# Low key halves on all 128 rows, a second gate ahead of the first branch product, and the mask step's minimum written into the statistics

## The chip, the cores and the metric

The kernel runs on one core of one Trainium2 chip. The metric is the device time of one execution in microseconds (us); lower is better. The version before takes 1885.06 us, the median of three runs (1883.31 to 1887.6). What a measurement of this kernel can tell from no change is about 0.2%, 3.8 us.

## The reference, cut to what matters

One decoder layer over 1024 tokens of width 1024, in float32. The part that the change touches is the mixer:

```python
s = einsum('nbqhgd,nbkhd->nbhgqk', qb, kw) * (dh ** -0.5)     # dh = 64, blocks of 128
s = where(mask, s, NEG_INF)
m = max(s, axis=-1)
if sink is not None: m = maximum(m, sk)                       # the sliding-window heads
p = exp(s - m[..., None])
denom = sum(p, axis=-1)                                       # + exp(sk - m) with a sink
o = einsum('nbhgqk,nbkhd->nbqhgd', p, vw) / denom
...
merged = sigmoid(ga) * ya + sigmoid(gb) * yb                  # ya, yb: branch products of the two attentions
y = einsum('btd,de->bte', merged, w_o)
```

There are 16 query heads of a sliding-window attention with two key heads and sinks (branch A), and 24 heads of a dilated attention in three patterns (branch B). A normalisation, a SwiGLU feed-forward part and a second normalisation follow.

## The kernel before, in words

**Products in three passes.** TensorE multiplies float32 operands as float32r, so every operand is split into a high part (ScalarE's copy, `w_hi`, `kh`, ...) and a low part (VectorE's difference, `w_lo`, `kl`, ...). A product is the three passes hi·hi, hi·lo, lo·hi; `mac`, with lines 137, 138 and 139, issues them for one 128x512 result.

**Stages.** The prologue (to about 77 us) makes the modulated input `u`. Stage 1 (to about 823 us) projects `u` and runs attention. Stage 2 (to about 1110 us) makes the gates, the branch products and their merge. Then follow `w_o`, the normalisation, and the feed-forward part. In each stage TensorE carries the work, in the order in which the Python code issues it; every other engine's queue, SyncE's DMA queue (SP) among them, is in program order as well.

**Stage 1.** `units` holds 12 units of branch B (a pair of heads and a pattern) and then 8 of branch A. `stream` is a generator of projections: per B unit a key projection (`k_stacks`), a value projection and a query projection, eight steps each; per A unit a query projection, and in the first of them the shared values and keys too. The main loop goes over the units' four parts (`subs`, 80 in all); in each it calls `scores`, pumps some steps of projection, calls `turn_probs` for the part before (transposes, line 544), `exponentials` (line 522), pumps more steps, and calls `weigh` for the part two back (line 567). So TensorE's projections for later units lie between the pieces of attention. `tasks` sends the B units' statistics off and fetches the weights that combine the three patterns.

**Key stacks.** When a key projection has been rotated, `k_stacks` makes for each of the two heads a tile `kh` of 128 rows: the high part of the key in the head's own 64 rows (line 448) and the same again in the other 64 rows (line 449), both by ScalarE. The query stack `qs` holds the query's high part in the head's own 64 rows and its low part in the other 64. One product `qs`·`kh` over 128 rows (line 495) is thus (q_hi + q_lo)·k_hi. The low key `kl` is made by VectorE in the head's own 64 rows only (line 454); the product over those 64 rows (line 501) adds q_hi·k_lo. Only branch A's shared keys have the low part in both halves (line 456).

**Scores.** Per part there are two blocks and two heads: four products of line 495, then four of line 501, the heads' halves in turn. They are 256 columns wide, or 128 where a block sees no block before it. Of the 80 groups 36 are all 256 wide, 28 have two blocks' products of each width, and 16 are all 128 wide. VectorE then scales, masks and takes the row maximum in one `tensor_tensor_reduce` for each head and block (line 507) into a small tile `mx`; a `tensor_scalar` for each head (line 514, with the sink's maximum line 512) negates it into the statistics `st`; ScalarE's exponential takes `st` as its bias.

**Stage 2.** `order` lists gates ("g") and branch products ("w"): gate 8, products 0 to 7, gate 9, product 8, gate 10, product 9, and so on. A gate is 48 matmuls of `u` and two pieces of `w_in`, then tanh (line 675) and a scale by VectorE (line 676). A branch product is 24 matmuls of `o_hl`, the split attention output, and one piece of weights. Gates 11, 12 and 13 are made in stage 1 and kept in `ga_d` in HBM; `make_gate` only fetches them. Ahead of gate 8, `ws.prepare(4)` splits four pieces of weights and `o_parts(0)` splits the first four parts of attention output; while gate 8 runs no weights are split. While a gate or product runs, `ws.step` splits the next piece and a step of `ada_steps` (a modulation by VectorE, line 826 and line 828) runs.

## Time and profile before

| | |
|---|---|
| median of three runs | 1885.06 us |
| profiled execution, its own time | 1886.68 us |
| its span in the trace | 1884.6 us |
| TensorE busy | 1827.5 us, 97% of the span |
| VectorE, ScalarE, GpSimd busy | 1154.8, 784.0, 600.0 us |
| mean granted TensorE clock | 0.992 |

PE is TensorE's matmul, PEld its weight load, DVE VectorE, ACT ScalarE, POOL GpSimd, SP SyncE. A row of the timeline gives the start, the time from first start to last end, engine, line, operation, output and inputs, size and count, and in brackets the idle time before it and what ended that. Matmuls overlap in their pipeline, so the distance of two starts tells what one costs, and the shown length does not.

### The profile page before, as it was taken

The page shows a single profiled execution, that of the slowest core. Times are in us where ns is not written, and L with a number is a line of the kernel's source. Part 1 is how long each engine was busy: PE and PEld are TensorE (multiplying, and loading weights), DVE is VectorE, ACT ScalarE, POOL GpSimd, SP SyncE. Part 2 cuts the span into 40 slices and gives each one's busy share as a digit, 9 for nine tenths or more (in the row PEclk, how much of TensorE's full clock was granted, in tenths as well). Part 3 has the DMA queues.
Part 4 walks back from the last instruction along what each step waited for, and adds up shares of the span by engine and source line. Part 5 has one row for each costly group of instructions (what it writes and reads, how often), then busy time and mean ns, then how long its engine had stood idle before and what let it go on. Part 6 is the DMA issues. An engine that isn't in the chain of part 4 may idle for free.

```text
span 1884.6 us, 24305 instructions
## 1 busy us (share of the span) xinstructions
PE 1827.5 (97%) x8924; PEld 1475.4 (78%) x8924; DVE 1154.8 (61%) x2136; ACT 784.0 (42%) x1664; POOL 600.0 (32%) x389
## 2 busy tenths in 40 slices
PE   6899999999999999989999999999999999999998
PEld 3678887877878767768888878878888888888886
DVE  5865567667667887643645365575565444674567
ACT  3544454544454667743112132653433333421122
POOL 2422323223223312100312242455664333531223
PEclk9999999999999999999999999999999999999999
DMA  8211112112111132144543223122222222442222
GB/s 280 91 34 35 35 36 79 40 39 76 42 57 63 41 95 76 57 168 155 208 137 137 79 72 134 57 90 101 85 78 85 89 79 89 151 134 71 97 84 89
DMA packets 72408, 171.85 MB, mean 91 GB/s; under 512 B 13089, under 2 KB 14177, under 8 KB 72290
## 3 DMA queue, kind: packets, MB, share of 16 engines
q1 hardware_dynamic: 71954, 169.26, 26.3%
q8 instruction: 70, 1.15, 0.3%
q0 software_dynamic: 336, 1.06, 0.2%
q14 instruction: 48, 0.39, 0.1%
HBM read 146.33 MB, written 23.95 MB: 90 GB/s over the span
## 4 chain that ended last, share of the span: by engine, by line
PE 81%; DVE 9%; ACT 4%; issue 3%; POOL 2%; DMA 1%; DVEq 0%; SPq 0%; POOLq 0%; ACTq 0%
PE pf L1108 22%; PE pj L137 7%; PE pj L139 7%; PE pj L138 6%; PE p L138 5%; PE p L139 5%; PE p L137 5%; PE pf L138 5%; PE pf L139 5%; PE pf L137 5%; PE pt L544 2%; PE po L567 2%; PE s L495 1%; PE s L501 1%; DVE probs L507 1%
## 5 line engine op out<-in xcount | busy, mean ns | idle before, releaser
L137 PE MATMUL pj<-u,w_hi 128*128 128x512 f32 x720 | 301.1, 418 | 0.0
L139 PE MATMUL pj<-u,w_lo 128*128 128x512 f32 x720 | 283.7, 394 | 0.0
L138 PE MATMUL pj<-u,w_hi 128*128 128x512 f32 x720 | 282.5, 392 | 0.0
L419 POOL TENSOR_TENSOR rb<-rb,sin_t 128x512 f32<-128x512 f32 x64 | 86.7, 1355 | 502.5 <-DVE rb L417 438.0
L118 DVE TENSOR_TENSOR w_lo<-r,w_hi 128x512 fp32r<-128x512 f32 x110 | 116.2, 1059 | 138.8 <-ACT w_hi L117 137.8
L79 DVE TENSOR_TENSOR w_lo<-w_raw,w_hi 128x512 fp32r<-128x512 f32 x148 | 131.2, 890 | 85.2 <-ACT w_hi L78 83.0
L522 ACT ACTIVATE probs<-probs,st 128x128 f32<-128x128 f32 (+1 forms) x320 | 146.0, 460 | 59.3 <-DVE st L512 30.1
L137 PEld LDWEIGHTS pj<-u,w_hi 128*128 128x128 f32 x720 | 136.2, 189 | 33.4 <-issue 4.7
L139 PEld LDWEIGHTS pj<-u,w_lo 128*128 128x128 f32 x720 | 135.8, 189 | 30.4
L138 PEld LDWEIGHTS pj<-u,w_hi 128*128 128x128 f32 x720 | 136.5, 190 | 22.4
L138 PE MATMUL pf<-wd,h 128*128 128x512 f32 x352 | 137.1, 389 | 0.0
L139 PE MATMUL pf<-wd,h 128*128 128x512 f32 x352 | 137.1, 389 | 0.0
L137 PE MATMUL pf<-wd,h 128*128 128x512 f32 x352 | 137.1, 389 | 0.0
L62 POOL TENSOR_TENSOR w_raw<-w_raw,gate 128x512 f32<-128x512 f32 x60 | 85.5, 1439 | 143.9 <-DMA w_raw<-in_w_down 120.6
L1327 DVE SCALAR_TENSOR_TENSOR zt<-zt,pf 128x512 f32<-128x512 f32 x112 | 75.3, 685 | 79.7 <-PE pf L139 79.7
L420 POOL TENSOR_TENSOR r<-ra,rb 128x512 f32<-128x512 f32 x63 | 114.5, 1817 | 6.1 <-DVE kl L454 1.3
L78 ACT ACTIVATE w_hi<-w_raw 128x512 fp32r<-128x512 f32 x148 | 90.8, 624 | 33.9 <-PE p L138 16.8
L546 ACT ACTIVATE ptsb<-pt 128x512 f32<-128x512 f32 (+1 forms) x128 | 63.5, 547 | 93.4 <-PE pt L544 93.0
L137 PE MATMUL p<-o_hl,w_hi 128*128 128x512 f32 x192 | 76.1, 396 | 6.8 <-ACT o_hl L117 6.8
L137 PE MATMUL p<-u,w_hi 128*128 128x512 f32 x208 | 82.2, 395 | 0.0
L139 PE MATMUL p<-u,w_lo 128*128 128x512 f32 x208 | 81.1, 390 | 0.0
L138 PE MATMUL p<-u,w_hi 128*128 128x512 f32 x208 | 81.0, 389 | 0.0
(305 smaller groups left out, 4266.8 us busy)
## 6 DMA issues: line engine op xcount, KB each, us to landing
w_raw<-in_w_in SPq DMA_DIRECT2D x116, 256.0 KB
r<-in_w_gate_up SPq DMA_DIRECT2D x47, 512.0 KB
a_raw<-in_w_ada SPq DMA_DIRECT2D x32, 512.0 KB
w_raw<-in_w_down SPq DMA_DIRECT2D x44, 256.0 KB
h_raw<-h_d SPq DMA_DIRECT2D x22, 512.0 KB
h_d<-g SPq DMA_DIRECT2D x40, 256.0 KB
wa<-in_w_ada_m SPq DMA_DIRECT2D x16, 512.0 KB
wb<-wt_d SPq DMA_DIRECT2D x24, 256.0 KB
```

Source lines behind the costliest of these rows:

```text
L62: self.nc.gpsimd.tensor_tensor(self.raws[i], self.raws[i], scale(), op=OP.mult)
L78: self.nc.scalar.activation(hi, raw, AF.Copy)
L79: self.nc.vector.tensor_tensor(lo, raw, hi, op=OP.subtract)
L118: nc.vector.tensor_tensor(lo, src, hi, op=OP.subtract)
L137: nc.tensor.matmul(ps, w[0], m[0], start=first, stop=False)
L138: nc.tensor.matmul(ps, w[0], m[1], start=False, stop=False)
L139: nc.tensor.matmul(ps, w[1], m[0], start=False, stop=last)
L419: eng.tensor_tensor(b, b, sin_t[:, s], op=OP.mult)
L420: eng.tensor_tensor(residue_half(res, r, t), by_residue(a, r), by_residue(b, r), op=OP.add)
L522: nc.scalar.activation(pr, pr, AF.Exp, bias=st[:, 0, h, b:b + 1], accum_out=st[:, 1, h, b:b + 1])
L1108: nc.tensor.matmul(ps, w[:, c], m[:, k], start=first and k == 0 and n == 0, stop=k == 3 and n == 2, skip_group_check=True)
L1327: nc.vector.scalar_tensor_tensor(z, z, ALPHA if gi == 0 else 1.0, pd, op0=OP.mult, op1=OP.add)
```

## The change

Five edits.

1. `k_stacks` makes the high and the low key in the head's own 64 rows only, and two DMAs on SP's queue copy each into the other 64 rows. ScalarE's second copy (line 449) and VectorE's line 456 are gone. `kl` is a tile for each head, with four buffers.
2. `scores` multiplies the whole `qs` of 128 rows by `kl`, so that a part has eight products of 128 rows; high and low stand next to each other for each head and block. This adds q_lo·k_lo to the sum.
3. The mask step scales by -QS and reduces by the minimum, straight into `st`. For branch A the negated sink (`nsinks`, made once) is the reduction's start. `mx` and the two `tensor_scalar` are gone.
4. The exponential takes its input times -1.
5. Gate 10 is made after gate 8, ahead of product 0, and written to `ga_d`; where it stood, it is fetched. Its two pieces of weights come earlier in the list. It runs no step of `ada_steps`.

```diff
+    bridge = 10
...
+        if i == 0:
+            order.append(("b", bridge))
         order.append(("w", i))
     for kind, i in order:
-        if kind == "g" and i not in made_early:
+        if kind == "b" or (kind == "g" and i not in (*made_early, bridge)):
             add_chunk(I["w_in"][gate_of[i]], 2, 4)
...
             kh = att.tile([P, T], F32R, name="kh", bufs=4)
+            kl = att.tile([P, T], F32R, name="kl", bufs=4)
             nc.scalar.activation(kh[own], res[own], AF.Copy)
-            nc.scalar.activation(kh[other], res[own], AF.Copy)
+            nc.sync.dma_start(kh[other].bitcast(F32), kh[own].bitcast(F32))
+            nc.vector.tensor_tensor(kl[own], res[own], kh[own], op=OP.subtract)
+            nc.sync.dma_start(kl[other].bitcast(F32), kl[own].bitcast(F32))
...
-                nc.tensor.matmul(pss[h][:, i, lo:], box["q"][h][:, b * P:(b + 1) * P],
-                                 khs[h][:, (b - 1 + lo) * P:(b + 1) * P], start=i == 0, stop=False,
-                                 skip_group_check=True)
-
-        for i, b, lo in blocks:
-            for h, own in enumerate((LO, HI)):
-                nc.tensor.matmul(pss[h][:, i, lo:], box["q"][h][own, b * P:(b + 1) * P],
-                                 kls[h][own, (b - 1 + lo) * P:(b + 1) * P], start=False, stop=i == 1,
-                                 skip_group_check=True)
+                for n, ks in enumerate((khs, kls)):
+                    nc.tensor.matmul(pss[h][:, i, lo:], box["q"][h][:, b * P:(b + 1) * P],
+                                     ks[h][:, (b - 1 + lo) * P:(b + 1) * P], start=i == 0 and n == 0,
+                                     stop=i == 1 and n == 1, skip_group_check=True)
...
-                    out=probs[:, h, i, lo:], in0=pss[h][:, i, lo:], in1=un["mask"][:, lo:], scale=QS, scalar=NEG,
-                    op0=OP.add, op1=OP.max, accum_out=mx[:, h, i:i + 1])
-            sl = slice(2 * qr, 2 * qr + 2)
-            if "kv" in un:
-                nc.vector.tensor_scalar(st[:, 0, h, sl], mx[:, h], un["sink"](h), -1.0, op0=OP.max, op1=OP.mult)
-            else:
-                nc.vector.tensor_scalar(st[:, 0, h, sl], mx[:, h], -1.0, None, op0=OP.mult)
+                    out=probs[:, h, i, lo:], in0=pss[h][:, i, lo:], in1=un["mask"][:, lo:], scale=-QS,
+                    scalar=un["sink"](h, nsinks) if "kv" in un else -NEG, op0=OP.add, op1=OP.min,
+                    accum_out=st[:, 0, h, b:b + 1])
...
-                nc.scalar.activation(pr, pr, AF.Exp, bias=st[:, 0, h, b:b + 1], accum_out=st[:, 1, h, b:b + 1])
+                nc.scalar.activation(pr, pr, AF.Exp, scale=-1.0, bias=st[:, 0, h, b:b + 1], accum_out=st[:, 1, h, b:b + 1])
...
-        if i in made_early:
+        if i in (*made_early, bridge) and not kept:
             nc.sync.dma_start(g, ga_d[i - 8])
             return
...
+        if kept:
+            nc.sync.dma_start(ga_d[i - 8], g)
...
+        if kind == "b":
+            make_gate(i, kept=True)
+            continue
```

How the engines' queues move is shown at two places. The first is ScalarE's queue where stage 2 begins; `o_hl` are the four first parts of attention output, `gt` the gates, `w_hi` pieces of weights, and in brackets stand the semaphores that an instruction waits for (DMASW: a DMA of GpSimd's queue). Before:

```order
L78 ACTIVATE w_hi<-w_raw 128x512 [waits DMAHW3_49]
L117 ACTIVATE o_hl<-o_raw 128x1024 [waits DMAHW2_49]
L117 ACTIVATE o_hl<-o_raw 128x1024 [waits DMAHW1_49,DMAHW0_49,DMAHW3_49,DVE_49,Activation_49]
L117 ACTIVATE o_hl<-o_raw 128x1024 [waits DMAHW6_49,DMASW3_49,Pool_49]
L117 ACTIVATE o_hl<-o_raw 128x1024 [waits DMAHW7_49,DMASW2_49,DMASW1_49]
L675 ACTIVATE gt<-p_7735 128x512 [waits PE_49]
L675 ACTIVATE gt<-p_7736 128x512 [waits PE_49]
L78 ACTIVATE w_hi<-w_raw 128x512 [waits DMAHW5_49]
```

The same place in the changed kernel; the first `w_hi` is here gate 10's last piece, the one after gate 8's two `gt` is product 0's:

```order
L78 ACTIVATE w_hi<-w_raw 128x512 [waits DMAHW7_49]
L117 ACTIVATE o_hl<-o_raw 128x1024 [waits DMAHW6_49,DMAHW5_49,DVE_49]
L117 ACTIVATE o_hl<-o_raw 128x1024 [waits DMAHW7_49]
L117 ACTIVATE o_hl<-o_raw 128x1024 [waits DMAHW4_49,DMAHW2_49,Activation_49]
L117 ACTIVATE o_hl<-o_raw 128x1024 [waits DMAHW3_49,DMASW3_49,Pool_49]
L666 ACTIVATE gt<-p_7533 128x512 [waits PE_49]
L666 ACTIVATE gt<-p_7534 128x512 [waits PE_49]
L78 ACTIVATE w_hi<-w_raw 128x512 [waits DMAHW1_49]
L666 ACTIVATE gt<-p_7594 128x512 [waits PE_49]
```

Since the tiles of stage 1 lie at other addresses, the fourth split and no longer the third and fourth waits for GpSimd's DMA; and product 0's weights, which were split ahead of the four `o_hl`, are split behind them and behind gate 8's tanh.

The second place is SP's queue where a pair of heads of branch B has had its three patterns (`wt_d` are the combining weights on their way to HBM, `wb` their fetch). Before:

```order
L650 DMA wt_d<-cst 8x16x8 x2
L55 DMA w_raw<-in_w_in 128x512 x2
L609 DMA wb<-wt_d 64x1024 x2
L55 DMA w_raw<-in_w_in 128x512
L584 DMA st_d<-sr 32x128
```

And in the changed kernel:

```order
L641 DMA wt_d<-cst 8x16x8 x2
L55 DMA w_raw<-in_w_in 128x512
L455 DMA kh<-kh 64x1024
L457 DMA kl<-kl 64x1024
L55 DMA w_raw<-in_w_in 128x512
L455 DMA kh<-kh 64x1024
L457 DMA kl<-kl 64x1024
L600 DMA wb<-wt_d 64x1024 x2
L55 DMA w_raw<-in_w_in 128x512
L575 DMA st_d<-sr 32x128
```

Four copies between halves now stand ahead of the fetch of the combining weights and beside the loads of projection weights; each waits for the engine that makes its source.

More of the change, by code (lines that the diff above doesn't have):

```diff
@@ L207, in decoder_layer @@
     sinks = tab.tile([P, 16], F32, name="sinks")
+    nsinks = tab.tile([P, 16], F32, name="nsinks")
     freq = tab.tile([P, 3], F32, name="freq")
@@ L356, in decoder_layer @@
     att = ph1.enter_context(tc.tile_pool(name="att", bufs=2, side="right", reuse_waits="tile"))
+    nc.vector.tensor_scalar(nsinks, sinks, -1.0, None, op0=OP.mult)
     mask_a, mask_b = mask[:, 0:3:2], mask[:, 1:3]
@@ L441, in q_stacks, with k_stacks @@
         return rotary(e, r, then)
-    def k_stacks(e, r, both, box):
+    def k_stacks(e, r, box):
         def stack(res, h):
@@ L447, in stack @@
             kh = att.tile([P, T], F32R, name="kh", bufs=4)
+            kl = att.tile([P, T], F32R, name="kl", bufs=4)
             nc.scalar.activation(kh[own], res[own], AF.Copy)
-            nc.scalar.activation(kh[other], res[own], AF.Copy)
+            nc.sync.dma_start(kh[other].bitcast(F32), kh[own].bitcast(F32))
+            nc.vector.tensor_tensor(kl[own], res[own], kh[own], op=OP.subtract)
+            nc.sync.dma_start(kl[other].bitcast(F32), kl[own].bitcast(F32))
             box.setdefault("kh", []).append(kh)
-            los = box.setdefault("kl", [])
-            if both or not los:
-                los.append(att.tile([P, T], F32R, name="kl", bufs=2))
-            nc.vector.tensor_tensor(los[-1][own], res[own], kh[own], op=OP.subtract)
-            if both:
-                nc.vector.tensor_tensor(los[-1][other], res[own], kh[own], op=OP.subtract)
-            elif h:
-                los.append(los[0])
+            box.setdefault("kl", []).append(kl)
         def then(res):
@@ L494, in scores @@
             for h in range(2):
-                nc.tensor.matmul(pss[h][:, i, lo:], box["q"][h][:, b * P:(b + 1) * P],
-                                 khs[h][:, (b - 1 + lo) * P:(b + 1) * P], start=i == 0, stop=False,
-                                 skip_group_check=True)
-        for i, b, lo in blocks:
-            for h, own in enumerate((LO, HI)):
-                nc.tensor.matmul(pss[h][:, i, lo:], box["q"][h][own, b * P:(b + 1) * P],
-                                 kls[h][own, (b - 1 + lo) * P:(b + 1) * P], start=False, stop=i == 1,
-                                 skip_group_check=True)
-        mx = att.tile([P, 2, 2], F32, name="mx", bufs=3)
+                for n, ks in enumerate((khs, kls)):
+                    nc.tensor.matmul(pss[h][:, i, lo:], box["q"][h][:, b * P:(b + 1) * P],
+                                     ks[h][:, (b - 1 + lo) * P:(b + 1) * P], start=i == 0 and n == 0,
+                                     stop=i == 1 and n == 1, skip_group_check=True)
         for h in range(2):
@@ L592, in keep_sums @@
         for h in range(2):
-            nc.scalar.activation(es[:, h], st[:, 0, h], AF.Exp, bias=un["sink"](h))
+            nc.scalar.activation(es[:, h], st[:, 0, h], AF.Exp, bias=un["sink"](h, sinks))
         nc.vector.tensor_tensor(es, es, st[:, 1], op=OP.add)
@@ L670, in decoder_layer @@
         units.append({"a": p, "kv": p // 4, "box": {}, "prev": see_prev[0], "mask": mask_a,
-                      "sink": lambda h, p=p: sinks[:, 2 * p + h:2 * p + h + 1]})
+                      "sink": lambda h, of, p=p: of[:, 2 * p + h:2 * p + h + 1]})
     progress = [0]
@@ L682, in stream @@
                 base, r = (p * 3 + g) * 3, B_DIL[g]
-                yield from k_stacks(base, r, False, un["box"])
+                yield from k_stacks(base, r, un["box"])
                 yield from values(base + 1, r, un["box"])
@@ L689, in stream @@
                     yield from values(37, 1, kv_a)
-                    yield from k_stacks(38, 1, True, kv_a)
+                    yield from k_stacks(38, 1, kv_a)
         for dc in tail_gates:
@@ L850, in decoder_layer, with make_gate @@
     gts = {}
-    def make_gate(i, *steps):
+    def make_gate(i, *steps, kept=False):
         g = mix.tile([P, T], F32, name="gt", bufs=2)
         gts[i] = g
-        if i in made_early:
+        if i in (*made_early, bridge) and not kept:
             nc.sync.dma_start(g, ga_d[i - 8])
@@ L859, in make_gate @@
         for n, t in enumerate(gemm_u(ps, ws.take(2), *steps)):
-            if n % 4 == 2:
+            if n % 4 == 2 and not kept:
                 next(ada, None)
```

## The prediction

> **What bounds the kernel now.** I read the page first, then the busy time in stretches, then the timeline of each place that the change touches.
>
> ```profile
> PE 1827.5 (97%) x8924; PEld 1475.4 (78%) x8924; DVE 1154.8 (61%) x2136; ACT 784.0 (42%) x1664; POOL 600.0 (32%) x389
> ```
>
> ```profile
> 89.00:290.00 201.00, 195.05 (x1048) 156.41 (x1046) 124.28 (x295) 97.56 (x235) 58.63 (x36) 0.97 0.11 36
> 636.00:700.00 64.00, 59.59 (x379) 44.30 (x375) 54.42 (x154) 44.55 (x126) 13.52 (x11) 1.00 0.26 80
> 700.00:823.00 123.00, 122.21 (x789) 93.97 (x783) 79.74 (x266) 86.20 (x253) 18.02 (x14) 1.00 0.22 73
> 823.00:846.00 23.00, 15.74 (x65) 12.34 (x66) 6.64 (x9) 7.15 (x10) 4.67 (x5) 0.87 0.71 247
> ```
>
> After the stretch's length stands TensorE's busy time. It works nearly without a pause, so two things can shorten the span: less matmul time, or the few places where it does idle. Those in reach of the change are 636 to 700 us (4.4 us idle, VectorE busy for 54 of 64), and above all 823 to 846 us (7.3 us idle, and a granted clock of 0.87). The long chain of feed-forward products gives the price of one matmul 512 wide:
>
> ```profile
> 1238.04 399.07 PE pf L1108 x1750
> ```
>
> That is 0.228 us each; a gate of 48 is 10.9 us.
>
> **Part 1: the second gate.** TensorE at the start of the branch products:
>
> ```profile
> 836.46 0.39 PE L139 MATMUL p<-o_hl,w_lo 128*128 128x512 f32 x1
> 843.65 0.80 PE L137 MATMUL p<-o_hl,w_hi 128*128 128x512 f32 x1 [6.80 <-ACT o_hl L117]
> 850.13 0.39 PE L138 MATMUL p<-o_hl,w_hi 128*128 128x512 f32 x1
> ```
>
> ```profile
> 839.80:850.00 10.20, 5.89 (x13) 4.37 (x14) 5.49 (x7) 4.09 (x6) 0.00 (x0) 0.50 0.25 89
> ```
>
> Product 0 does the first two parts of `o_hl`, then waits for the third, and after the wait the clock stands at 0.50 until 850. Between 836.46 and 850.13 us 14 matmuls start (13 in the window, one at 836.46), worth 3.2 us; 10.5 of the 13.7 us are lost. The Trainium skill ("TensorE: Matmul & The Clock Gate", Part 1) puts the way back to full clock at about 3.4 us of sustained work. Here it took 6.5 us from 843.65, at half speed; by the page about 1.5 us less would hang on it. The row decides.
>
> Gate 10 now fills this hole. Product 0 began 12 matmuls ahead of 836.69, at 833.95; gate 10 starts there and ends at 844.85. What then ends last is not the `o_hl` but product 0's weights, which the change puts behind them:
>
> ```profile
> 842.54 2.00 ACT L117 ACTIVATE o_hl<-o_raw 128x1024 fp32r<-128x1024 f32 x2 [10.31 <-DMA oa_d<-o]
> 844.45 1.06 ACT L675 ACTIVATE gt<-p 128x512 f32<-128x512 f32 x2
> 845.40 0.63 ACT L78 ACTIVATE w_hi<-w_raw 128x512 fp32r<-128x512 f32 x1
> ```
>
> ```profile
> 843.63 2.36 DVE L118 TENSOR_TENSOR o_hl<-o_raw,o_hl 128x1024 fp32r<-128x1024 f32 x2 [10.15 <-ACT o_hl L117]
> 845.90 0.42 DVE L676 TENSOR_SCALAR gt<-gt 128x512 f32<-128x512 f32 x1
> 846.24 0.75 DVE L826 TENSOR_SCALAR acc<-a_raw,c_act 128x1024 f32<-128x1024 f32 x1
> 847.24 0.68 DVE L79 TENSOR_TENSOR w_lo<-w_raw,w_hi 128x512 fp32r<-128x512 f32 x1
> ```
>
> In the new queue only one split is late. ScalarE: 842.54 + 1.0 + 1.06 + 0.63 = 845.2 for `w_hi`. VectorE: 843.63 + 1.18 + 0.42 + 0.75 + 0.42 + 0.68 = 847.1 for `w_lo`. TensorE's third matmul of product 0 needs `w_lo`; unhindered it would start at 844.85 + 0.46 = 845.3. So 1.8 us stay idle, in two pieces. From 636 to 700 us 4.4 us of pauses left the clock at 1.00, so I count no half clock. Gain: 10.5 - 1.8 = **8.7 us**, between 10.5 (weights in time) and 4 (a new pause of 5 us with some half clock).
>
> Where gate 10 stood, five products now follow each other instead of four. Each takes 24 x 0.228 = 5.5 us and one piece of weights, and VectorE's and ScalarE's shares (0.68 and 0.63 us a piece) fit many times. The gate's write and its fetch are one transfer each on SP; the fetch waits for GpSimd to release gate 8's tile, as those of gates 11 to 13 wait, and is first read a product later. I count nothing, and 1 us if that cover is gone. Two steps of `ada_steps` come later; they have work ahead of them either way.
>
> **Part 2: the score products.** A group 256 wide, with the matmuls around it, and its fourth product by a narrow window:
>
> ```profile
> 806.59 0.40 PE L139 MATMUL pj<-u,w_lo 128*128 128x512 f32 x1
> 806.83 0.63 PE L495 MATMUL s<-kh,qs 128*128 128x256 f32 x4
> 807.39 0.50 PE L501 MATMUL s<-kl,qs 64*128 64x256 f32 x4
> 808.39 0.40 PE L139 MATMUL pj<-u,w_lo 128*128 128x512 f32 x1
> ```
>
> ```profile
> 807.18 0.28 PE L495 MATMUL s<-kh,qs 128*128 128x256 f32 x1
> ```
>
> The four 128-row products are (807.18 - 806.83) / 3 = 0.117 us apart. To the first 64-row product it is 0.21 us, so the change of height costs 0.09. The whole way from one line 139 to the next is 1.80 us. With eight 128-row products it would be 0.24 + 8 x 0.117 + 2 x 0.228 = 1.64: 0.16 less. Groups 128 wide, and with both widths:
>
> ```profile
> 183.20 0.40 PE L139 MATMUL pj<-u,w_lo 128*128 128x512 f32 x1
> 184.86 0.40 PE L139 MATMUL pj<-u,w_lo 128*128 128x512 f32 x1
> ```
>
> ```profile
> 138.38 0.40 PE L139 MATMUL pj<-u,w_lo 128*128 128x512 f32 x1
> 138.79 0.45 PE L495 MATMUL s<-kh,qs 128*128 128x256 f32 x2
> 140.17 0.40 PE L139 MATMUL pj<-u,w_lo 128*128 128x512 f32 x1
> ```
>
> ```profile
> 809.32 1.04 PE L544 MATMUL pt<-ident,probs 128*128 128x128 f32 x8
> ```
>
> Eight transposes 128 wide last 1.04 us, of which the last one's length is about 0.27, so they are 0.11 apart. All 128 wide: 0.24 + 8 x 0.11 + 0.46 = 1.58 against 1.66, 0.08 less. Both widths: 0.24 + 4 x 0.11 + 4 x 0.117 + 0.46 = 1.61 against 1.79, 0.18 less. The sum is 36 x 0.16 + 28 x 0.18 + 16 x 0.08 = 12.1 us. Some groups begin with a wait that the saving doesn't shorten, and the way back to the 512-wide products may keep some hundredths each: I take **10 us**, between 12.1 and 3.
>
> The Trainium skill ("TensorEngine Tiling (Array Packing)", sections Theoretical Speedup and Key Properties) speaks for the old form: contracting 64 rows, two tiles run side by side, up to twice as fast. It also says that changing the mode drains the array. The trace agrees with the second; by the first alone the four low products would take the time of two, which the rows don't show: 0.43 us from 807.39 to the next projection matmul, 0.11 each.
>
> **Part 3: ScalarE's second copy.** Where a pair of heads ends (about 290, 424 and 558 us), TensorE waits twice for ScalarE:
>
> ```profile
> 288.09 1.06 ACT L449 ACTIVATE kh<-r 64x1024 fp32r<-64x1024 f32 x1
> 290.19 0.85 ACT L546 ACTIVATE ptsb<-pt 128x384 f32<-128x384 f32 x2
> ```
>
> ```profile
> 290.71 0.29 PE L581 MATMUL pt<-ident,st 128*32 128x128 f32 x1 [0.88 <-ACT ptsb L546]
> 293.31 0.66 PE L474 MATMUL pt<-ident,vt 128*128 128x128 f32 x4 [0.93 <-ACT vt L478]
> ```
>
> The key stacks stand in ScalarE's queue ahead of `ptsb` and `vt`, and two of their four copies, 2.1 us, go. That is more than either pause: 3 x (0.88 + 0.93) = 5.4 us at most, 0 at least if VectorE's statistics are late next. I take **4.5 us**. Elsewhere these copies lie beside matmuls and are worth nothing.
>
> **Part 4: the mask step.** Two `tensor_scalar` a part go:
>
> ```profile
> L514 DVE TENSOR_SCALAR st<-mx 128x2 f32<-128x2 f32 x96 | 44.0, 459 | 3.3
> L512 DVE TENSOR_SCALAR st<-mx,sinks 128x2 f32<-128x2 f32 x64 | 27.2, 425 | 2.3
> ```
>
> 71 us of VectorE, mostly beside matmuls. They count where the next scores wait for the banks that the mask step reads:
>
> ```profile
> PEld s L495 <- DVE mx L507: 7.4, 13, 1.1
> ```
>
> TensorE's own idle time from 636 to 823 us is 4.4 + 0.8 = 5.2 us; most of it is where VectorE also combines patterns. I take **2.5 us**, between 0 and 5.2. The minimum in place of the maximum, the sink as a start value and the exponential's factor are other settings of the same instructions: nothing.
>
> **Part 5: the copies by DMA.** 52 transfers of 256 KB are new on SP's queue. The nearest rows for their landing, in us at the end, are GpSimd's:
>
> ```profile
> vt<-wa_d POOLq DMA_DIRECT2D x2, 256.0 KB, 5.2
> ...
> oa_d<-o POOLq DMA_DIRECT2D x1, 512.0 KB, 3.6
> ```
>
> In every other unit of branch B the value and query projections, 16 steps of six matmuls, lie between the key stack and its first score, over 20 us at 0.228 us a matmul. Tight is the first unit, where VectorE ends last:
>
> ```profile
> 87.26 3.43 DVE L454 TENSOR_TENSOR kl<-r,kh 64x1024 fp32r<-64x1024 f32 x2
> 95.85 0.98 PE L495 MATMUL s<-kh,qs 128*128 128x128 f32 x3 [0.81 <-DVE qs L434]
> ```
>
> The second low key is ready at 90.7; a landing 5.2 us later is 95.9, just when its product is due. Behind a waiting copy in SP's queue stand weight loads, three pieces ahead of their use, and at a boundary the combining weights, for which VectorE waits. I take **2 us lost**, between 0 and 8.
>
> **Sum.** 8.7 + 10 + 4.5 + 2.5 - 2 = 23.7 us. The profiled execution took 1886.68 us by its own clock, so 1863.0; it lies 1.6 us above the median of the runs, so 1861.4 us.
>
> **The rivals.**
>
> *Slower: full-height low products that don't keep the pace.* In the group with both widths, two 256-wide products last 0.45 us together, one alone 0.28: they start 0.17 apart, not 0.117. If eight that load the same weights twice run at 0.17, a group is 0.24 + 8 x 0.17 + 0.46 = 2.06, 0.26 longer than the 1.80 now; 80 times that is 21 us lost in place of 10 gained, 1861.4 + 31 = 1892. It turns the sign from 0.16 us a product on. Against it: three distances at 0.117, with other weights each time. Chance 0.06.
>
> *The 64-row pairs were worth their rows.* If four low products at full height cost 2 x 0.117 = 0.23 us more a group than half height, 18 us are lost in place of 10 gained: 1889. The Tiling page's speedup rule would have it so; the rows (0.11 a product) speak against. Chance 0.03.
>
> *SP's queue becomes the bound.* The four copies ahead of `wb` make VectorE wait a landing longer, 3.6 us by the shorter of the rows, at three boundaries, and TensorE behind it, and the 4.5 us there are lost too: 1861.4 + 15 = 1877. For it: SP's queue is in order. Against: VectorE has slack there. Chance 0.12.
>
> *The gate doesn't cover the hole.* If the first split were the late one, all four (4 x 1.18 us) stand ahead of the weights, the pause is 5.4 us and may bring the half clock: 5.5 us less gain, 1867. Against: the new queue shows GpSimd's DMA at the fourth. Chance 0.12.
>
> My forecast keeps 0.67. Its own range is 1852 (all upper ends but the landing) to 1871; with the SP rival the range is 1852 to 1877. A measurement of this kernel can tell about 0.2%, 3.8 us, from no change. Faster 0.89, same 0.04, slower 0.07.
>
> **What would show it.** TensorE's idle time at the first branch product under 2 us and no half clock near it; score groups 1.6 us from line 139 to line 139; no `[0.9 <-ACT` at 290, 424 and 558; the first score not later after its query stack than now. The prediction is wrong if score products stand over 0.13 us apart, if the clock still falls at the first product, or if new waits for `kh`, `kl` or `wb` sum to over 8 us.

## The result, and the profile after

| | before | changed |
|---|---|---|
| median | 1884.32 us (4 runs, 1883.31 to 1887.6) | 1864.36 us (4 runs, 1861.09 to 1866.62) |
| span of the profiled execution | 1884.6 us | 1862.2 us |

The ratio is 0.989 (95% interval 0.987 to 0.9909). The change is faster, by 20.0 us between the medians and 22.4 between the two profiled spans. The forecast was 1861.4. The total is near, but the terms of its sum are not: the gain at the boundaries did not come, the score products brought some six tenths of theirs, and the mask step brought more than twice its own.

The page of the changed kernel first, the row that answers to the first one of the prediction. The columns are busy time, share of the span and count.

```profile
PE 1811.9 (97%) x8924; PEld 1480.5 (80%) x8924; DVE 1094.8 (59%) x1975; ACT 756.3 (41%) x1638; POOL 601.7 (32%) x389
```

TensorE issues the same 8924 matmuls in 15.6 us less busy time, and VectorE's busy time falls by 60 us. Next the stretches that answer to the four of before (the program is some 7 us ahead by 629 us, and 14 by 809). After the length stand TensorE's busy time, weight loads, VectorE, ScalarE, GpSimd, then the granted clock, the DMA engines' share and GB/s.

```profile
89.00:288.00 199.00, 193.48 (x1062) 159.22 (x1061) 108.51 (x267) 91.56 (x238) 58.85 (x36) 0.98 0.25 66
629.00:693.00 64.00, 60.50 (x389) 47.84 (x384) 50.18 (x132) 44.55 (x125) 13.29 (x11) 1.00 0.28 81
693.00:809.00 116.00, 116.00 (x769) 94.88 (x768) 69.06 (x225) 83.83 (x246) 18.01 (x14) 1.00 0.23 77
809.00:832.00 23.00, 22.57 (x100) 18.28 (x99) 8.19 (x12) 8.41 (x13) 4.71 (x5) 1.00 0.73 250
```

The last row is the hole before the branch products: 7.3 us idle at a clock of 0.87 before, 0.43 us idle at 1.00 now; the row ends inside the one pause that is left there, which is shown below. In the third row TensorE is never idle.

Counted by milestones in the two traces, the 22.4 us come from three places. Branch B (from its first score to branch A's first) took 533.3 us and takes 526.4: 6.9. Branch A (from there to the first matmul of gate 8) took 195.0 us and takes 188.1: 7.0. From the first matmul of gate 8 to the last one of the branch products it was 289.6 us and is 281.0: 8.6. What follows took 772.0 us and takes 772.1. About 1.7 us of branch B's 6.9 are not the change's. Both executions run at half clock after the prologue's end, and the length of that differs: the window from 99.50 to 102.30 us of before, and then the same window of after, show it.

```profile
99.50:102.30 2.80, 2.80 (x8) 2.17 (x7) 1.16 (x1) 1.61 (x5) 1.13 (x1) 0.50 0.00 0
```

```profile
99.50:102.30 2.80, 2.80 (x14) 2.31 (x13) 0.42 (x1) 1.51 (x2) 1.25 (x1) 1.00 0.00 0
```

The stretch lasts 10.24 us in before and 6.83 in after, and the 1.7 are half of the difference, an estimate. Among the other executions, ones that don't touch this place show either length. Where the stretch falls counts too: two of the runs below have the changed kernel's stage 1 to the letter (gate 10 where it stood, product 0's weights ahead), and their first unit of branch B takes 43.0 and 43.2 us against 41.9.

**The first branch product.** TensorE's timeline of the changed kernel at the end of gate 10:

```profile
830.77 0.39 PE L139 MATMUL p<-u,w_lo 128*128 128x512 f32 x1
831.00 0.40 PE L137 MATMUL p<-o_hl,w_hi 128*128 128x512 f32 x1
831.24 0.40 PE L138 MATMUL p<-o_hl,w_hi 128*128 128x512 f32 x1
832.61 0.50 PE L139 MATMUL p<-o_hl,w_lo 128*128 128x512 f32 x1 [0.97 <-DVE w_lo L79]
```

Product 0 follows the gate at once, and one pause is left, 832.61 - 831.24 - 0.23 = 1.14 us, ended by VectorE's `w_lo` as forecast.

**A group of scores, all 256 wide**, in the changed kernel:

```profile
793.04 0.40 PE L139 MATMUL pj<-u,w_lo 128*128 128x512 f32 x1
793.27 0.28 PE L497 MATMUL s<-kh,qs 128*128 128x256 f32 x1
793.39 0.27 PE L497 MATMUL s<-kl,qs 128*128 128x256 f32 x1
793.50 0.28 PE L497 MATMUL s<-kh,qs 128*128 128x256 f32 x1
...
794.09 0.28 PE L497 MATMUL s<-kl,qs 128*128 128x256 f32 x1
...
794.68 0.39 PE L139 MATMUL pj<-u,w_lo 128*128 128x512 f32 x1
```

Eight products stand (794.09 - 793.27) / 7 = 0.117 us apart, and from line 139 to line 139 it is 1.64 us: both to the digit of the forecast. Where transposes follow the scores in place of a projection, the group is shorter by 0.11 to 0.12 only. Over all 80 groups, by their kind, that makes 10.3 us of TensorE.

**The boundary at 290 us.** The two pauses for ScalarE are gone, and others stand there. First TensorE, then VectorE, then SP's queue of the changed kernel:

```profile
292.93 0.39 PE L139 MATMUL pj<-u,w_lo 128*128 128x512 f32 x1
294.06 0.55 PE L535 MATMUL pt<-ident,probs 128*128 128x128 f32 x3 [0.74 <-DVE v L476]
295.26 0.55 PE L535 MATMUL pt<-ident,probs 128*128 128x128 f32 x3 [0.65 <-DVE v L476]
```

```profile
292.18 1.23 DVE L645 TENSOR_TENSOR o<-o,wb 128x1024 f32<-128x1024 f32 x1 [5.84 <-DMA wb<-wt_d]
293.32 0.68 DVE L476 COPY v<-pt 128x512 f32<-128x512 f32 x1
```

```profile
281.23 0.47 SPq L455 DMA_DIRECT2D kh<-kh  x1
282.51 0.47 SPq L457 DMA_DIRECT2D kl<-kl  x1
...
283.73 0.59 SPq L455 DMA_DIRECT2D kh<-kh  x1
284.42 0.54 SPq L457 DMA_DIRECT2D kl<-kl  x1
285.01 2.28 SPq L600 DMA_DIRECT2D wb<-wt_d  x2
```

The four copies stand right ahead of the combining weights `wb`. VectorE waits 5.84 us for `wb`, and the value copies that TensorE needs stand behind that in VectorE's queue. In before the same two steps were these, from SP's queue and from VectorE's:

```profile
288.14 1.15 SPq L609 DMA_DIRECT2D wb<-wt_d  x2
```

```profile
293.48 1.23 DVE L654 TENSOR_TENSOR o<-o,wb 128x1024 f32<-128x1024 f32 x1 [1.76 <-DMA wb<-wt_d]
```

There the combining step began 5.34 us after the fetch was issued (293.48 - 288.14); now it is 7.17 (292.18 - 285.01), 1.83 longer. VectorE comes to the step 5.38 us earlier than before (286.34 against 291.72), but the fetch is issued only 3.13 earlier, right behind the second `kl`. That makes 2.25 us, and with the 1.83 the 4.08 by which the wait has grown. The whole program is 3.91 us ahead here (the unit's first score starts at 266.44 against 270.35); the rest of the 5.38 is VectorE's own gain. A third pause, for `qs`, follows near 313 us, and all three return near 426 and 559 us. The waits of TensorE's queue from 270 to 625 us in the changed kernel (total us, times, longest):

```profile
PE pt L535 <- DVE v L476: 3.7, 6, 0.7
PE s L497 <- DVE qs L439: 2.2, 3, 0.8
```

They sum to 5.9 us; the pauses that went had 5.4.

### The profile page after: what moved, and what is told of

It is laid out like the page before. It is cut to its first block, busy times and chain, and to the rows that moved or that the text cites. A ratio compares the mean times of both kernels' runs of the same rounds, so it can differ in the third digit from the quotient of the medians.

```text
span 1862.2 us, 24287 instructions
## 1 busy us (share of the span) xinstructions
PE 1811.9 (97%) x8924; PEld 1480.5 (80%) x8924; DVE 1094.8 (59%) x1975; ACT 756.3 (41%) x1638; POOL 601.7 (32%) x389
## 4 chain that ended last, share of the span: by engine, by line
PE 80%; DVE 8%; ACT 3%; issue 3%; DMA 2%; POOL 2%; SPq 0%; DVEq 0%; ACTq 0%; POOLq 0%
PE pf L1104 21%; PE pj L137 7%; PE pj L139 7%; PE pj L138 7%; PE pf L139 5%; PE pf L137 5%; PE pf L138 5%; PE p L138 5%; PE p L139 5%; PE p L137 5%; PE s L497 3%; PE po L558 2%; PE pt L535 2%; DMA wb<-wt_d 1%; POOL r L425 1%
## 5 line engine op out<-in xcount | busy, mean ns | idle before, releaser
L137 PE MATMUL pj<-u,w_hi 128*128 128x512 f32 x720 | 295.5, 410 | 0.0
L138 PE MATMUL pj<-u,w_hi 128*128 128x512 f32 x720 | 281.9, 392 | 0.0
L137 PEld LDWEIGHTS pj<-u,w_hi 128*128 128x128 f32 x720 | 135.9, 189 | 27.2 <-issue 4.6
L497 PE MATMUL s<-kh,qs 128*128 128x256 f32 (+1 forms) x320 | 80.4, 285 | 10.4 <-issue 5.5
```

The source lines that it names most:

```text
L137: nc.tensor.matmul(ps, w[0], m[0], start=first, stop=False)
L138: nc.tensor.matmul(ps, w[0], m[1], start=False, stop=False)
L497: nc.tensor.matmul(pss[h][:, i, lo:], box["q"][h][:, b * P:(b + 1) * P], ks[h][:, (b - 1 + lo) * P:(b + 1) * P], start=i == 0 and n == 0, ...
```

## The experiments

The theory drawn from this had four parts: the gate fills the hole (8.6 us); the score products bring about 10; the boundary's gain was lost to `wb`; the mask step brings about 3. Each experiment undoes or mends one part. The first four ran on one chip beside before at 1885.86 us, the next three beside 1886.39, the last three beside 1885.54. The changed kernel's own ratio has an interval of about 3.7 us to either side, so differences from it under 4 us rest on the trace, not on the time. Taken by the ratios to before in place of the medians, the differences below change by up to 1.3 us.

### The combining weights fetched ahead of the copies

```diff
             combine_weights(last["b"][0])
+            fetch_bcast((last["b"][0], 0), wt_d[last["b"][0], 0])
...
-            if i < 3:
+            if 0 < i < 3:
                 fetch_bcast((p, i), wt_d[p, i])
```

> The changed kernel, with the first fetch of a pair's combining weights (wb) sent as soon as the weights are on their way to HBM, ahead of the four key copies in SP's queue, not behind them. Theory: at the three boundaries of branch B the copies hold wb back, VectorE waits 5.8 us for it, and TensorE waits for VectorE at three places (0.74, 0.65 and 0.70 us); all that goes, 3 x 2.1 = 6 us less than the changed kernel's 1864, so about 1858. Rival: VectorE is late there by its own work, or the copies load the DMA engines however the queue stands: within 1 us of 1864, with the same waits in the trace.

Measured: 1858.63 us (1856.38 to 1859.46), ratio 0.9854 [0.984, 0.9867]; 5.7 us faster than the changed kernel. VectorE's row at the boundary carries no wait:

```profile
284.96 1.20 DVE L645 TENSOR_TENSOR o<-o,wb 128x1024 f32<-128x1024 f32 x1
```

TensorE has no pause with a named cause from 270 to 625 us. So the wait for `wb` was the cause of all nine pauses, and its price, 5.7 us by the time, is more than the 4.5 that the forecast had wanted to gain there. In the trace branch B gains 6.8 us (519.6 against 526.4), and 2.9 are lost again from gate 8 to the last branch product. Product 0 has a second pause here, for `w_hi`, and this time the half clock does follow (TensorE's timeline, and a window):

```profile
822.88 0.50 PE L137 MATMUL p<-o_hl,w_hi 128*128 128x512 f32 x1 [0.53 <-ACT w_hi L78]
824.58 0.50 PE L139 MATMUL p<-o_hl,w_lo 128*128 128x512 f32 x1 [0.97 <-DVE w_lo L79]
```

```profile
825.30:828.60 3.30, 3.30 (x10) 2.52 (x9) 2.30 (x4) 0.00 (x0) 0.00 (x0) 0.50 0.79 196
```

### All four copies made by the engines again

```diff
             nc.scalar.activation(kh[own], res[own], AF.Copy)
-            nc.sync.dma_start(kh[other].bitcast(F32), kh[own].bitcast(F32))
+            nc.scalar.activation(kh[other], res[own], AF.Copy)
             nc.vector.tensor_tensor(kl[own], res[own], kh[own], op=OP.subtract)
-            nc.sync.dma_start(kl[other].bitcast(F32), kl[own].bitcast(F32))
+            nc.vector.tensor_tensor(kl[other], res[own], kh[own], op=OP.subtract)
```

> The changed kernel, with the other halves of kh made by ScalarE and those of kl by VectorE; no key copies by DMA. Theory: at the boundaries the wait for wb goes (6 us less), ScalarE's pauses of the kernel before come back (0.9 + 0.9 us at three boundaries, 5.4 us more), so 1863 to 1865, with ScalarE and no longer VectorE named as the releaser at 290, 424 and 558 us. Rival: the DMA copies cost more than at the boundaries (first unit, weight loads): 1858 or less. Rival: they cost nothing and ScalarE's copies do: about 1870.

Measured: 1865.93 us, ratio 0.9894 [0.9881, 0.9908]: the same as the changed kernel. The waits of TensorE from 270 to 625 us (total us, times, longest):

```profile
PE pt L475 <- ACT vt L479: 4.1, 3, 1.4
PE pt L572 <- ACT ptsb L537: 2.7, 3, 0.9
```

These are the pauses of before with the same causes, 6.8 us in place of 5.4. So the DMA copies did take ScalarE's pauses away, and gave about as much back through `wb`. The fetch of `wb` and its use stand 5.34 us apart here, 291.17 - 285.83, as in before:

```profile
285.83 1.14 SPq L600 DMA_DIRECT2D wb<-wt_d  x2
```

```profile
291.17 1.23 DVE L645 TENSOR_TENSOR o<-o,wb 128x1024 f32<-128x1024 f32 x1 [1.27 <-DMA wb<-wt_d]
```

The other price stands ahead of the first score, once. VectorE makes both halves of two `kl` there, 1.22 us more for each, ahead of `qs`, and TensorE is idle for 7.44 us in place of the changed kernel's 4.93:

```profile
95.68 0.44 PE L497 MATMUL s<-kh,qs 128*128 128x128 f32 x1 [7.44 <-DVE qs L439]
```

So beside copies on the engines, the DMA copies are worth 2.5 us in the first unit.

### Low products over 64 rows again

```diff
-                for n, ks in enumerate((khs, kls)):
-                    nc.tensor.matmul(pss[h][:, i, lo:], box["q"][h][:, b * P:(b + 1) * P],
-                                     ks[h][:, (b - 1 + lo) * P:(b + 1) * P], start=i == 0 and n == 0,
-                                     stop=i == 1 and n == 1, skip_group_check=True)
+                nc.tensor.matmul(pss[h][:, i, lo:], box["q"][h][:, b * P:(b + 1) * P],
+                                 khs[h][:, (b - 1 + lo) * P:(b + 1) * P], start=i == 0, stop=False,
+                                 skip_group_check=True)
+        for i, b, lo in blocks:
+            for h, own in enumerate((LO, HI)):
+                nc.tensor.matmul(pss[h][:, i, lo:], box["q"][h][own, b * P:(b + 1) * P],
+                                 kls[h][own, (b - 1 + lo) * P:(b + 1) * P], start=False, stop=i == 1,
+                                 skip_group_check=True)
```

> The changed kernel, with the low products over the head's own 64 rows again, four high products and then four low ones as in the kernel before; the copies stay, so kl's other half is made and not read (q_lo*k_lo is left out, as in the kernel before). Theory: the score groups grow by 0.16, 0.175 and 0.08 us where projections follow and by 0.11 and 0.12 us where transposes follow, 10.3 us in all: about 1874.5. Rival (64-row pairs pass two at a time and are cheaper than full height; the gain came from elsewhere): 1864 or less.

Measured: 1870.88 us, ratio 0.9921 [0.9909, 0.9934]: 6.5 us slower than the changed kernel, so the half-height form is the dearer one, but not by 10. The group as the timeline of this kernel has it, from 64-row products to the projection:

```profile
799.03 0.63 PE L496 MATMUL s<-kh,qs 128*128 128x256 f32 x4
799.59 0.50 PE L501 MATMUL s<-kl,qs 64*128 64x256 f32 x4
800.02 0.50 PE L137 MATMUL pj<-u,w_hi 128*128 128x512 f32 x1
```

The four low products take 800.02 - 799.59 = 0.43 us; four at full height, 0.117 apart, take 0.47. The 0.04 that half height saves is lost to the change of height, 0.09 ahead of them as the prediction read it, and again behind them: the first projection matmul takes 0.34 us to the next start, where 0.24 is usual after a full-height group. The low products do start in pairs, one of each head; at 799.60 us, 0.01 after the first one's start, two have begun (a narrow window of the same timeline):

```profile
799.59 0.39 PE L501 MATMUL s<-kl,qs 64*128 64x256 f32 x2
```

But a pair takes 0.21 to 0.22 us, where two full-height products take 0.23. The Trainium skill ("TensorEngine Tiling (Array Packing)", Theoretical Speedup) gives two tiles side by side up to twice the rate. At this kernel's sizes no such gain is seen. By the trace, branch B loses 4.9 us and branch A 2.4, and some 1.1 of the 4.9 lie in the first unit and are the half clock's place, by the 43.0 against 41.9 above; a slower TensorE also leaves VectorE more time before it is waited for.

### Gate 10 where it stood

```diff
-        if i == 0:
-            order.append(("b", bridge))
...
-        if kind == "b" or (kind == "g" and i not in (*made_early, bridge)):
+        if kind == "b" or (kind == "g" and i not in made_early):
...
-        if i in (*made_early, bridge) and not kept:
+        if i in made_early and not kept:
```

> The changed kernel, with gate 10 at its old place. Theory: the wait of 7 us ahead of the third part of the attention output and the half clock behind it come back, 8.6 us more: about 1873. Rival: with other addresses only the last of the four splits is late, so the first three parts of product 0 cover part of the hole: 4 to 6 us more, 1869. Rival: the gate was only moved and is paid elsewhere: within 2 us of 1864.

Measured: 1871.9 us, ratio 0.9927 [0.9914, 0.9941]: 7.5 us slower. The hole is back, and the half clock with it (windows, and TensorE's timeline, of this kernel):

```profile
827.00:834.00 7.00, 3.86 (x8) 2.77 (x9) 4.35 (x6) 3.67 (x7) 0.00 (x0) 0.51 0.09 19
```

```profile
829.67 0.79 PE L137 MATMUL p<-o_hl,w_hi 128*128 128x512 f32 x1 [3.94 <-ACT o_hl L117]
...
833.66 0.57 PE L138 MATMUL p<-o_hl,w_hi 128*128 128x512 f32 x1
834.07 0.39 PE L139 MATMUL p<-o_hl,w_lo 128*128 128x512 f32 x1
```

In the trace the stretch from gate 8 to the last branch product is 6.8 us longer than with the gate ahead. The way back to full clock took from 829.67 to 834.07, 4.4 us.

### The old mask step

```diff
-                    out=probs[:, h, i, lo:], in0=pss[h][:, i, lo:], in1=un["mask"][:, lo:], scale=-QS,
-                    scalar=un["sink"](h, nsinks) if "kv" in un else -NEG, op0=OP.add, op1=OP.min,
-                    accum_out=st[:, 0, h, b:b + 1])
+                    out=probs[:, h, i, lo:], in0=pss[h][:, i, lo:], in1=un["mask"][:, lo:], scale=QS, scalar=NEG,
+                    op0=OP.add, op1=OP.max, accum_out=mx[:, h, i:i + 1])
+            sl = slice(2 * qr, 2 * qr + 2)
+            if "kv" in un:
+                nc.vector.tensor_scalar(st[:, 0, h, sl], mx[:, h], un["sink"](h, sinks), -1.0, op0=OP.max, op1=OP.mult)
+            else:
+                nc.vector.tensor_scalar(st[:, 0, h, sl], mx[:, h], -1.0, None, op0=OP.mult)
```

> The changed kernel, with the old mask step: maximum into mx, a tensor_scalar for each head into st, the exponential without a factor. Theory: VectorE's 71 us come back; in the stretch of branch A, where the next scores wait for VectorE, TensorE loses about 3 us, elsewhere nothing: about 1867.5. Rival: VectorE's time lies beside matmuls everywhere: within 1 us of 1864.4. Rival: the accumulated statistics shorten the way to the exponentials in all 80 parts: 5 us or more.

Measured: 1872.27 us (1872.08 to 1875.54), ratio 0.9931 [0.9918, 0.9943]: 7.9 us slower, far over the theory's 3. Branch A takes 194.1 us in place of 188.1. Set beside the changed kernel matmul by matmul, a steady unit of branch A is longer by 0.67 us, and 0.53 of that arise at one place, the unit's last group of scores:

```profile
735.68 0.28 PE L498 MATMUL s<-kh,qs 128*128 128x256 f32 x1
735.80 0.28 PE L498 MATMUL s<-kl,qs 128*128 128x256 f32 x1
736.36 0.39 PE L498 MATMUL s<-kh,qs 128*128 128x256 f32 x1 [0.28 <-DVE mx L503]
```

This group comes 4.7 us after another that is 256 wide; the others have 6.5 us, or follow the group with both widths. Its third product, the first of the second bank, waits until VectorE has left that bank. The wait returns in each steady unit. In the changed kernel the place has no wait.

### The mask step alone, the score products alone

The first of these is the kernel before with edits 3 and 4; the second is the kernel before with edits 1 and 2. After the first seven runs it was open whether the parts add up.

```diff
-                    out=probs[:, h, i, lo:], in0=pss[h][:, i, lo:], in1=un["mask"][:, lo:], scale=QS, scalar=NEG,
-                    op0=OP.add, op1=OP.max, accum_out=mx[:, h, i:i + 1])
...
+                    out=probs[:, h, i, lo:], in0=pss[h][:, i, lo:], in1=un["mask"][:, lo:], scale=-QS,
+                    scalar=un["sink"](h, nsinks) if "kv" in un else -NEG, op0=OP.add, op1=OP.min,
+                    accum_out=st[:, 0, h, b:b + 1])
```

> The kernel before with the new mask step alone (the minimum into the statistics, no separate tensor_scalar). Theory: the parts add up, since undoing the gate (7.5), the score products (6.5) and the mask step (7.9) one at a time from the changed kernel costs 21.9 us together, and the whole change brings about 21.5. Then the mask step alone brings 6 to 8 us: about 1878 where before takes 1885. Rival: with the old, slower score groups TensorE leaves VectorE enough time, so the mask step is worth at most the 2.5 us of the forecast: 1882 or more, and the 7.9 came only because the new score groups had made VectorE late.

Measured: 1880.29 us (1877.32 to 1880.62), ratio 0.9965 [0.9953, 0.9978], 5.3 us faster than before. That lies between the two expectations. Branch A falls from 195.0 to 189.7 us, 5.3; the wait at the last group is gone there too. Branch B gains 1.9 us, and 1.1 are lost at the hole ahead of the branch products, which this kernel still has.

```diff
+            nc.sync.dma_start(kh[other].bitcast(F32), kh[own].bitcast(F32))
...
+                for n, ks in enumerate((khs, kls)):
+                    nc.tensor.matmul(pss[h][:, i, lo:], box["q"][h][:, b * P:(b + 1) * P],
+                                     ks[h][:, (b - 1 + lo) * P:(b + 1) * P], start=i == 0 and n == 0,
+                                     stop=i == 1 and n == 1, skip_group_check=True)
```

> The kernel before with the new key stacks and full-height score products alone: old mask step, no gate ahead of the first branch product. Theory (the parts add up): 5 to 7 us faster than before, about 1879, not the 10.3 that the shorter score groups show in the trace, because in branch A the old mask step's pause at the scores takes a part of it back, and at the three boundaries the wait for the combining weights stands in place of ScalarE's. Rival: the 10.3 us are whole in it, 1875 or less. Other rival: the old mask step takes all of it, 1883 or more.

Measured: 1879.65 us (1878.7 to 1880.31), ratio 0.9965 [0.9952, 0.9979], 5.9 us faster than before, as the theory had it. Branch B gains 4.6 us, branch A only 0.4. The last groups of one steady unit, in before and then here:

```profile
740.85 0.28 PE L495 MATMUL s<-kh,qs 128*128 128x256 f32 x1
741.31 0.61 PE L495 MATMUL s<-kh,qs 128*128 128x256 f32 x3 [0.18 <-DVE mx L507]
```

```profile
759.64 0.28 PE L496 MATMUL s<-kh,qs 128*128 128x256 f32 x1
...
760.32 0.39 PE L496 MATMUL s<-kh,qs 128*128 128x256 f32 x1 [0.28 <-DVE mx L501]
```

In before the second bank's product starts 0.46 us after the first product in place of 0.12. Here it starts 0.68 us after it in place of 0.24, so the wait has grown from 0.34 to 0.44. TensorE saves 0.11 us in each of the other groups and gives a part back at the one where VectorE is late; 0.27 us a steady unit is left. In the second and third unit, where VectorE also combines patterns, it gives back more: they take 25.6 and 27.2 us against 24.5 and 26.6 in before.

### One copy on VectorE

```diff
-            nc.sync.dma_start(kl[other].bitcast(F32), kl[own].bitcast(F32))
+            nc.vector.tensor_tensor(kl[other], res[own], kh[own], op=OP.subtract)
```

> The changed kernel with the second copy of kl made by VectorE instead of a DMA: two transfers of 256 KB ahead of the combining weights in place of four. At the first boundary the combining step starts 7.2 us after the first of its two weight transfers is issued; before, and with all copies on the engines, 5.1 to 5.3. Theory (the load on the DMA engines delays the landing): about half the delay goes, the combining step starts near 6.2 us after the issue, the pauses at each boundary shrink from 2.1 us to 1 or less: 2 to 4 us faster than the changed kernel, about 1861. Rival (order on the queue alone): the landing keeps 7 us, the pauses stay, and the time is the changed kernel's, 1864. Other rival: VectorE's 2.4 us more a unit cost what they cost elsewhere, and it is slower, 1866 or more.

Measured: 1868.57 us (1867.3 to 1872.91), ratio 0.9912 [0.9899, 0.9926], 4.2 us slower than the changed kernel. The landing did as the first theory said, the time did not. SP's queue and VectorE's:

```profile
286.89 1.45 SPq L600 DMA_DIRECT2D wb<-wt_d  x2
```

```profile
292.99 1.23 DVE L645 TENSOR_TENSOR o<-o,wb 128x1024 f32<-128x1024 f32 x1 [2.60 <-DMA wb<-wt_d]
```

From issue to use it is 6.10 us: between 5.34 with no copies and 7.17 with four. But VectorE's two copies a unit, 2.4 us, now delay the mask step, the exponentials wait for it, and `vt` stands behind them in ScalarE's queue:

```profile
288.78 0.40 ACT L513 ACTIVATE probs<-probs,st 128x128 f32<-128x128 f32 x1 [2.48 <-DVE st L502]
```

```profile
291.18 0.66 PE L475 MATMUL pt<-ident,vt 128*128 128x128 f32 x4 [2.31 <-ACT vt L479]
```

TensorE waits 2.31 us for `vt` at each boundary, 6.9 in all, only 1.0 more than the changed kernel's 5.9. Two other prices come with it. Ahead of the first score TensorE is idle for 7.37 us in place of 4.93, as with all copies on the engines; and behind the first pause for `vt` this execution runs at half clock for 3.41 us (from 291.86). So the boundary has three chains of nearly equal length, and shortening one by work put on another engine moves the pause there.

### Product 0's weights ahead of the attention output, and the best of both

```diff
         if kind == "b":
-            make_gate(i, kept=True)
+            make_gate(i, (5,), kept=True)
...
                 ws.prepare(4)
+                if i == 8:
+                    make_gate(i, ())
+                    ws.step()
                 parts = o_parts({8: 0, 9: 1, 17: 2}[i])
-                make_gate(i, ())
+                if i != 8:
+                    make_gate(i, ())
```

> The changed kernel, with gate 8 issued ahead of the four splits of attention output, and product 0's weights split between the two, so that they no longer stand behind the late fourth split. Theory: the pause of 1.14 us at product 0's third matmul goes: 1863.2. Rival: the first three splits, now behind gate 8's tanh, or the fourth, are late in its place: 1864.4 or more.

Measured: 1862.1 us (1860.61 to 1863.31), ratio 0.9873 [0.9858, 0.9888], 2.3 us faster than the changed kernel; the two intervals overlap, so the time alone does not settle it. The pause is gone in the trace: from 829.96 to 835.40 us product 0's 24 matmuls follow each other, 5.44 us. `w_lo` was what they waited for. From gate 8 to the last branch product it is 1.9 us less than in the changed kernel.

The last kernel holds this edit and that of the first experiment.

> The changed kernel with both edits: the first fetch of the combining weights ahead of the key copies, and product 0's weights ahead of the splits. Theory: the gains add, 5.8 + 1.1 us: 1857.5. Rival: the second edit gains nothing beside the first: 1858.6.

Measured: 1855.27 us (1854.34 to 1856.01), ratio 0.9835 [0.9822, 0.9849]: 9.1 us faster than the changed kernel, 29 to 31 faster than before. It beats both. The two gains by themselves sum to 8.0 us, and 1.1 more is within what these times can tell; but the trace has a reason for it, since product 0's half clock and its pause for `w_hi` in the first experiment's kernel are gone here. One pause is left there, 0.56 us for the split attention output.

## Why the prediction was right, and where it was not

**Part 1, the gate: right.** Forecast 8.7 us, 8.6 in the trace, 7.5 by undoing it. What ends last was named rightly (`w_lo`), the pause is 1.14 in place of 1.8 us, and in this execution no half clock follows it. That last point is in part luck. The prediction counted none because 4.4 us of pauses from 636 to 700 us had left the clock at 1.00. In the run with gate 10 where it stood the same stretch has 3.41 us at 0.50, from 666.78; and in the first experiment's run the pause at product 0, with one of 0.53 us ahead, was followed by 3.41 us too. The gate moved, with its write and its fetch, added no wait of its own at the products. The rival in which the gate does not cover the hole is out.

**Part 2, the score products: right in size per group, too large in the sum.** The distance of 0.117 us and the 1.64 us a group came as forecast, and 10.3 us of TensorE went. The kernel gets 5.9 of them alone and 6.5 beside the others. The step "I take 10 us" had reckoned with waits at the start of some groups that the saving doesn't shorten. The one that mattered stands inside a group, in each unit of branch A. That the old mask step takes it back is shown by the run with the scores alone, where branch A gains 0.4 us. With the 64-row products back beside the new mask step, TensorE's pauses from 270 to 625 us sum to 4.3 us in place of 5.9, so there too a part of the saving had gone into waits. Both rivals about full height are out: products stand 0.17 apart only right behind a change of width, and the 64-row form costs 6.5 us more. The prediction read the old low products as 0.11 us each; they start in pairs, 0.21 to 0.22 us from one pair to the next, which changes nothing in its sum.

**Part 3, ScalarE's second copy: failed.** The forecast had 4.5 us for "two of their four copies, 2.1 us, go. That is more than either pause". That is true of ScalarE, whose pauses went. What is late next was said to be VectorE's statistics at worst; it was `wb`. The prediction had this as the rival in which SP's queue becomes the bound, with a chance of 0.12 and a price of 15 us. It came true as a mechanism at 5.7 us, what the first experiment gives back. VectorE waits 4.1 us longer for `wb` (5.84 against 1.76), more than the 3.6 of the rival; a part of that is slack, as the prediction said against it, and TensorE is left with pauses about as long as before's.

Is it the order in SP's queue or the load on the DMA engines? From 283 to 291 us the engines' share is 0.99 in the changed kernel and 0.25 in before. The way from issue to use grows with the copies, 5.34, 6.10 and 7.17 us for none, two and four. Counted from the unit's first score (270.35 us in before, 266.44 in the changed kernel), the 4.1 us are 1.83 of longer way, 0.78 of later issue, and 1.47 by which VectorE itself comes sooner. Counted in the same way against the run with all copies on the engines (267.41), the fetch is issued only 0.15 us later, since it stands behind a load of weights there, but used 1.98 later. So the load is the greater part of what the copies did, and the place in the queue is little; fetching ahead of the copies mends both. This split is worked out, not run. A transfer of a few bytes in the copies' place, which would keep the order without the load, was not tried.

**Part 4, the mask step: the term was mis-sized.** Forecast 2.5 us between 0 and 5.2; alone it brings 5.3, and undone beside the others it costs 7.9. The step "I take 2.5 us" halved TensorE's idle time in branch A, on the reasoning that the rest belongs to the combining of patterns. A rest does stay: with the mask step alone 2.1 us of the 5.2 are left (189.71 us of branch A, 187.64 busy), nearly all in the second and third unit, where patterns are combined. What failed is the measure. Idle time as the windows count it is less than what a wait costs, since the lengths of matmuls overlap: a steady unit of before shows 0.18 us idle, and with the mask step alone it is 0.52 us shorter. The term also looked at branch A alone, and branch B gains 1.9 us. And the bound of 5.2 was taken from a TensorE as slow as before's; one that is faster by the score groups waits longer for the same VectorE, 7.2 us of branch A with the scores alone (194.61 us, 187.41 busy).

**Part 5, the copies by DMA: right where it looked, wrong where it did not.** The first score starts at 94.67 us, 94.59 in before, so the first unit lost nothing; with the low halves made by VectorE in place of the copies it loses 2.5 us. The price came at the boundaries, which this part mentions in a clause.

**The sum.** The forecast was 23.7 us. With what undoing showed in the place of each term it is 7.5 + 6.5 + 0 + 7.9 - 0 = 21.9, and measured were 20.0, which is as near as medians of this kernel tell. From the other side, the mask step's 5.3 and the scores' 5.9 alone make 18.7 with the 7.5 of the gate. So the parts add up within what these times tell. Gate and scores came 1.2 and 3.5 us under the forecast, the boundary 4.5 under, the mask step 5.4 and the copies 2 over. The errors nearly cancel, so the hit on the total is in good part luck and says less than the parts. The range's slow end of 1871 is not worked out in the prediction: all lower ends together (4 + 3 + 0 + 0 - 8) would give 1886.

## What to carry to other kernels

Where an engine's pause is taken away by DMA copies, look at what stands behind them on that queue, what load they put on its transfers, and who waits for it: fetching that ahead was worth more than the copies. Two savings on engines that wait for each other are not to be sized one at a time: the slower engine's saving is bounded by the wait that will be there after the other's, not by the one in the profile now. And a hole with a known length is best filled with work that is ready, with the weights of what follows put ahead of the filling.

## What the runs showed of the hardware

- Four copies of 256 KB from 64 partitions to the other 64, with the weight loads and the next fetch among them, kept the 16 DMA engines busy at 0.99 for 8 us, and lengthened the way of the next 512 KB from issue to use from 5.34 to 7.17 us.
- In the changed kernel a pause of 1.14 us (0.97 idle) left the granted clock at 1.00. In the first experiment's run the same pause, with 0.53 us idle shortly ahead, was followed by 3.41 us at 0.50; in the run with the low products over 64 rows it came with 0.64 idle ahead and was not. After a pause of 3.94 us, with shorter ones around it, the clock was 0.51, and the way back was 4.4 us. The stretch at half clock after the prologue was 6.83 us in some executions and 10.24 in others. The Trainium skill ("TensorE: Matmul & The Clock Gate", Part 1) has a free-running activity window of about 3.4 us and says that the way back varies from run to run with its phase. The lengths agree with that grid (3.41, twice and three times it), but the two after the prologue are longer than the one window that the page charges.
- Four products 256 wide over 64 rows, in alternating halves, took 0.43 us, and four over 128 rows 0.47. The two halves' products started within 0.01 us of each other, and the pairs 0.21 to 0.22 us apart. The changes of height on both sides cost 0.09 and 0.10 us.
